# Attention tiles of a mixer layer: one bias-and-minimum pass, one cast and one subtraction per tile over shared PSUM rows, normalising a tile later, some loads in another order

## The chip, the cores and the metric

The kernel runs on one core of one Trainium2 chip. The metric is the device time of one execution in microseconds (us); lower is better. The time before is the median of three runs.

## The reference, cut to what matters

One layer of a hybrid backbone over 2048 latent tokens (a 32 x 64 grid, 1024 channels) and 256 context tokens, in float32. After a norm and modulation, one input projection gives eight column groups. Four of them feed neighbourhood attention with 8 heads of 64 channels: every latent query sees a clamped 8 x 16 window of the grid, with a learned bias, and all context keys, in one softmax:

```python
s_loc = einsum('bhrqd,bhrkd->bhrqk', qr, kg) * scale + bias[None]
s_loc = where(mask, s_loc, -inf)
s_ctx = einsum('bhrqd,bhcd->bhrqc', qr, k_ctx) * scale
p = softmax(concatenate([s_loc, s_ctx], axis=-1), axis=-1)
o = einsum('bhrqk,bhrkd->bhrqd', p_loc, vg) + einsum('bhrqc,bhcd->bhrqd', p_ctx, v_ctx)
y_na = merge(o) * silu(na_g)
```

The other four groups feed a retention path. Both results go through one output projection, a gated residual and a final norm.

## The kernel before, in words

The program has three stages. From 0 to about 562 us it makes the modulation and the projections of keys, values, gates and queries, and stores them in DRAM. From 562 to 1068 us it runs the attention, and fills the gaps of TensorE with projections of the retention path (the "fill": `fill(n)` advances a generator by n steps of three or six matmuls, lines L351 and L362). After that come the retention and the output projection.

The attention has 128 tiles: 8 heads h, 4 row blocks i, 4 column blocks j, tile number t = 16h + 4i + j, and 128 queries in each. A tile has nk = 288, 384 or 512 local keys (12 or 16 grid rows by 24 or 32 grid columns) and 256 context keys. Every float32 operand of a matmul is kept as a high and a low part (`hl`), so each product is made of two or three matmuls. The loop `for t in range(NT + 3)` (L958) writes each engine's order out by hand, as a software pipeline:

- `s_mm(t)`: TensorE makes the scores, local ones in `pl` (two buffers), context ones in `pc`, one PSUM tile of two halves that tiles t and t+1 share.
- a third of the fill, then `s_min(t)`: VectorE copies the context scores to SBUF with their minimum (L752), then adds the bias to the local ones with the minimum of both (L754). Scores carry the opposite sign, so the minimum stands for the softmax's maximum.
- `p_tr(t-2)`: TensorE transposes the probabilities of tile t-2 into `tl` and `tcx` (L773, L776), and ScalarE casts both to the high part in `pt` (L778, L779).
- `s_exp(t)`: ScalarE takes the exponential with its sum (L759).
- `p_lo(t-2)`: VectorE subtracts to get the low part (L786, L787).
- `s_norm(t)`: VectorE takes the reciprocal of the sum (L764), GpSimd multiplies the tile by it (L765).
- a third of the fill, `pv(t-3)`: the products with the values into `po` (L797, L799). On every second tile `combine` adds the four quarters of `po`: ScalarE copies one half (L817), VectorE adds (L818), GpSimd adds twice more (L821), and at the end of a row block of an odd head GpSimd multiplies by the gate (L825).
- the rest of the fill, then, for later tiles, the biases on GpSimd (`bias`, L719 and L722) and the loads.

All loads of this stage are issued by one queue, that of SyncE (SP), in program order: queries (`load_q`, L697), keys (L683), eight groups of value rows per head with six buffers (`load_v`, L705, four transfers a group), gates (`load_gate`, L807), biases (L691), and the fill's own: weights (`st`, L169), rotary tables (L405 and L435) and two reloads of spilled blocks (`hhi`, `hlo`, L673). A load that waits for its buffer holds up all that stand behind it. Stores are issued by ScalarE's queue. The order of the value loads stands in a table:

```python
for g in {(0, 1): (3,), (0, 3): (4,), (1, 1): (5,), (1, 3): (6,), (2, 3): (7,)}.get((i, j), ()):
    load_v(hd, (g,))
```

Group 3 takes the buffer of group 5 of the head before, which that head's last tile reads in its `pv`, three iterations after its scores.

Of the kernel before, what the change touches and what calls it, by code (L numbers as in the profile page):

```python
# [76 lines left out]
def hybrid_kernel(ctx: ExitStack, tc: tile.TileContext, a: dict, out: bass.AP):  # L77
# [526 lines left out]
    psl = pool(pax, "psl", 2, space=PSUM)  # L604
    psc = pool(pax, "psc", 1, space=PSUM)

# [73 lines left out]
    def load_head(h):  # L680
# [6 lines left out]
        return dict(k2=k2, vh=vh, vc=vc, nb={}, vt={}, q={})  # L687
# [25 lines left out]
    def bias(hd, rt, ct):  # L713
# [7 lines left out]
        t = mp.tile([P, kr, cw], F32, name=f"nb{int(rt == 1)}{ct}")  # L721
        nc.gpsimd.tensor_tensor(t, mcol[:, ct, ec:ec + cw].unsqueeze(1).to_broadcast([P, kr, cw]),  # L722
                                hd["ep"][:, :, ec:ec + cw], ALU.subtract)
        hd["nb"][rt, ct] = t
# [7 lines left out]
    def s_mm(t):  # L732
        h, i, j, kr0, kr, kc0, cw = dims(t)
        hd, nk = heads[h], kr * cw
        if t % 2 == 0:
            tl_st["pc"] = psc.tile([P, 2, LC], F32, name="pc")
        pc = tl_st["pc"][:, t % 2, :]
        pl = psl.tile([P, 512], F32, name="pl")
# [5 lines left out]
        sp = ap_.tile([P, 768], F32, name="sp", bufs=3)  # L744
        st = ap_.tile([P, 4], F32, name="stt", bufs=4)
        tl_st[t] = dict(pl=pl, pc=pc, sp=sp, st=st, nk=nk)

    def s_min(t):
        h, i, j = dims(t)[:3]
        T = tl_st[t]  # L750
        sp, st, nk = T["sp"], T["st"], T["nk"]
        nc.vector.tensor_scalar(sp[:, nk:nk + LC], T["pc"], 1.0, None, ALU.mult, ALU.min, accum_out=st[:, 0:1])  # L752
        nb = heads[h]["nb"][RTYPE[i], CTYPE[j]].rearrange("p a b -> p (a b)")
        nc.vector.tensor_tensor_reduce(sp[:, :nk], T["pl"][:, :nk], nb, 1.0, st[:, 0:1], ALU.add, ALU.min, st[:, 1:2])  # L754

    def s_exp(t):
        T = tl_st[t]
        sp, st, n = T["sp"], T["st"], T["nk"] + LC
        nc.scalar.activation(sp[:, :n], sp[:, :n], AF.Exp, bias=st[:, 1:2], scale=-1.0, accum_out=st[:, 2:3])  # L759

    def s_norm(t):
        T = tl_st[t]
        sp, st, n = T["sp"], T["st"], T["nk"] + LC
        nc.vector.reciprocal(st[:, 3:4], st[:, 2:3])  # L764
        nc.gpsimd.tensor_scalar(sp[:, :n], sp[:, :n], st[:, 3:4], 0.0, ALU.mult, ALU.add)  # L765

    def p_tr(t):
# [3 lines left out]
        tl = psl.tile([P, 4, P], F32, name="tl", bufs=1)  # L771
        for g in range(ng_):
            nc.tensor.transpose(tl[:cn, g, :], sp[:, g * cn:(g + 1) * cn], ident)  # L773
        tcx = psc.tile([P, 2, P], F32, name="tcx")
        for g in range(2):
            nc.tensor.transpose(tcx[:, g, :], sp[:, nk + g * P:nk + (g + 1) * P], ident)  # L776
# [3 lines left out]
        T.update(tl=tl, tcx=tcx, pt=pt)  # L780

    def p_lo(t):
        h, i, j, kr0, kr, kc0, cw = dims(t)
        T = tl_st[t]
        pt, ng_, cn = T["pt"], kr // 4, 4 * cw
        nc.vector.tensor_tensor(pt[:cn, :ng_, 1, :], T["tl"][:cn, :ng_, :], f(pt)[:cn, :ng_, 0, :], ALU.subtract)  # L786
        nc.vector.tensor_tensor(pt[:, 4:, 1, :], T["tcx"], f(pt)[:, 4:, 0, :], ALU.subtract)  # L787

    def pv(t):
        h, i, j, kr0, kr, kc0, cw = dims(t)  # L790
        T, hd = tl_st[t], heads[h]
        pt, ng_, cn = T["pt"], kr // 4, 4 * cw
# [557 lines left out]
```

## Time and profile before

| | |
|---|---|
| three runs, median (lowest to highest) | 1419.59 us (1414.53 to 1420.13) |
| profiled execution, first to last instruction | 1413.8 us |
| TensorE busy | 1346.2 us (95%) |
| VectorE, ScalarE, GpSimd busy | 670.2, 553.4, 614.5 us |
| attention stage, 562 to 1068 us: TensorE busy | 473.38 of 506 us |

The profile is of one execution. The page gives its span and no other time of it; the median of the runs lies 5.8 us above the span, for what lies around the first and the last instruction and for the spread between runs. Busy time is that of each engine's instructions; idle time is put down to what ended it.

### The profile page before, as it was taken

How to read it: one execution, taken by the hardware profiler on the slowest of the kernel's cores; microseconds unless marked ns; L12 is line 12 of the kernel's file. 1: busy time of each engine (PE TensorE's matmuls, PEld its weight loads, DVE VectorE, ACT ScalarE, POOL GpSimd, SP SyncE). 2: the span in 40 equal slices, each digit the busy share in tenths (PEclk: the TensorE clock that was granted, in tenths of full speed). 3: DMA queues.
4: the chain of work that ended last, by engine and by line, in shares of the span. 5: the costliest groups of instructions: out<-in, count | busy, mean ns of one | idle time of the engine just before them, and what ended most of it. 6: DMA issues, size and time to landing. Idle time of an engine off the chain costs nothing.

```text
span 1413.8 us, 23044 instructions
## 1 busy us (share of the span) xinstructions
PE 1346.2 (95%) x8380; PEld 1175.6 (83%) x8380; DVE 670.2 (47%) x1563; ACT 553.4 (39%) x1283; POOL 614.5 (43%) x703
## 2 busy tenths in 40 slices
PE   6989999999999999999899988798999999999997
PEld 2467899988887888998799878598999879888886
DVE  5786111100021131677777767577673644344445
ACT  4454212212212221765466544356563234333332
POOL 4452302112201221676777746477673155454342
PEclk9999999999999999999999999999999999999999
DMA  9543666233244577557557585847436997555433
GB/s 310 168 164 133 215 219 231 92 110 104 90 147 159 202 266 218 141 156 196 158 155 174 162 241 167 227 124 191 134 115 203 295 310 258 188 168 174 154 117 127
DMA packets 203634, 253.20 MB, mean 179 GB/s; under 512 B 13057, under 2 KB 151425, under 8 KB 202498
## 3 DMA queue, kind: packets, MB, share of 16 engines
q1 hardware_dynamic: 168098, 186.98, 45.2%
q10 hardware_dynamic: 35424, 64.76, 12.7%
q8 instruction: 66, 1.08, 0.3%
q14 instruction: 46, 0.38, 0.1%
HBM read 168.86 MB, written 82.84 MB: 178 GB/s over the span
## 4 chain that ended last, share of the span: by engine, by line
PE 73%; DMA 10%; DVE 8%; ACT 3%; POOL 2%; issue 2%; SPq 1%; ACTq 0%; DVEq 0%; POOLq 0%
PE mm L351 24%; PE mm L362 19%; PE mm L1193 11%; PE po L797 2%; PE tl L773 2%; PE pl L742 2%; PE mm L916 2%; DMA t<-in_rot_s_dram 2%; DMA q<-qS 2%; PE pc L743 1%; PE po L799 1%; PE tcx L776 1%; PE mm L295 1%; DMA t<-in_rot_k_dram 1%; PE mm L1105 1%
## 5 line engine op out<-in xcount | busy, mean ns | idle before, releaser
L351 PE MATMUL mm<-hhi,whi 128*128 128x512 f32 x640 | 259.6, 406 | 0.0
L351 PE MATMUL mm<-hlo,whi 128*128 128x512 f32 x640 | 253.4, 396 | 5.6 <-DVE hlo L264 2.2
L351 PE MATMUL mm<-hhi,wlo 128*128 128x512 f32 x640 | 253.3, 396 | 0.3 <-DVE wlo L332 0.3
L362 PE MATMUL mm<-whi,hhi 128*128 128x256 f32 x768 | 224.6, 292 | 0.0
L362 PE MATMUL mm<-wlo,hhi 128*128 128x256 f32 x768 | 216.7, 282 | 2.7 <-POOL wlo L332 2.7
L362 PE MATMUL mm<-whi,hlo 128*128 128x256 f32 x768 | 216.1, 281 | 0.0
L332 POOL TENSOR_TENSOR wlo<-st,whi 128x256 fp32r<-128x256 f32 (+1 forms) x97 | 112.4, 1176 | 225.4 <-ACT whi L330 225.2
L765 POOL TENSOR_SCALAR sp<-sp,stt 128x640 f32<-128x640 f32 (+2 forms) x128 | 103.6, 810 | 105.4 <-DVE stt L764 79.6
L362 PEld LDWEIGHTS mm<-wlo,hhi 128*128 128x128 f32 x768 | 145.0, 189 | 3.4 <-POOL wlo L332 3.3
L351 PEld LDWEIGHTS mm<-hlo,whi 128*128 128x128 f32 x640 | 120.8, 189 | 31.3 <-issue 3.3
L362 PEld LDWEIGHTS mm<-whi,hhi 128*128 128x128 f32 x768 | 145.2, 189 | 1.1
L362 PEld LDWEIGHTS mm<-whi,hlo 128*128 128x128 f32 x768 | 145.3, 189 | 0.0
L351 PEld LDWEIGHTS mm<-hhi,whi 128*128 128x128 f32 x640 | 120.9, 189 | 29.1 <-issue 4.6
L351 PEld LDWEIGHTS mm<-hhi,wlo 128*128 128x128 f32 x640 | 120.5, 188 | 29.4 <-DVE wlo L332 0.7
L759 ACT ACTIVATE sp<-sp,stt 128x640 f32<-128x640 f32 (+2 forms) x128 | 107.9, 843 | 51.8 <-DVE stt L754 51.3
L778 ACT CAST pt<-tl 96x384 fp32r<-96x384 f32 (+3 forms) x128 | 67.9, 531 | 150.6 <-PE tl L773 137.2
L786 DVE TENSOR_TENSOR pt<-tl,pt 96x384 fp32r<-96x384 f32 (+3 forms) x128 | 79.4, 620 | 44.5 <-ACT pt L778 43.8
L1193 PE MATMUL mm<-wor,y 128*128 128x512 f32 x384 | 95.6, 398 | 1.5 <-DVE xt L1202 1.1
L742 PE MATMUL pl<-k,q 128*128 128x384 f32 (+2 forms) x256 | 83.3, 346 | 7.1 <-DMA q<-qS 7.1
L1193 PE MATMUL mm<-won,y 128*128 128x512 f32 x336 | 89.9, 406 | 0.0
L743 PE MATMUL pc<-k,q 128*128 128x256 f32 x256 | 72.1, 286 | 16.8 <-DVE sp L752 16.7
L1193 PEld LDWEIGHTS mm<-wor,y 128*128 128x128 f32 x384 | 69.9, 188 | 17.7 <-issue 3.4
(220 smaller groups left out, 2639.1 us busy)
## 6 DMA issues: line engine op xcount, KB each, us to landing
st<-in_w_in_dram SPq DMA_DIRECT2D x48, 512.0 KB
q<-qS SPq DMA_DIRECT2D x64, 256.0 KB
vS<-o ACTq DMA_DIRECT2D x18, 512.0 KB
k<-kS SPq DMA_DIRECT2D x16, 576.0 KB
kS<-o SPq DMA_DIRECT2D x16, 512.0 KB
woS<-g ACTq DMA_DIRECT2D x32, 256.0 KB
qS<-o ACTq DMA_DIRECT2D x16, 512.0 KB
vt<-vS SPq DMA_DIRECT2D x128, 64.0 KB
```

What stands on the lines that cost most here:

```text
L332: eng.tensor_tensor(l, r, f(h), ALU.subtract)
L351: nc.tensor.matmul(pm[:, :n], ww[:, k, cs], h[:, k, :], start=(k == 0 and i == 0), stop=(k == KC - 1 and i == 2))
L362: nc.tensor.matmul(pm[:, t * WG:(t + 1) * WG], h[:, k, o:o + P], ww[:, k, :], start=(k == 0 and i == 0), stop=(k == KC - 1 and i == 2))
L742: nc.tensor.matmul(pl[:, :nk], qa, kg[:, kr0:kr0 + kr, kc0:kc0 + cw], start=(hl == 0), stop=(hl == 1))
L743: nc.tensor.matmul(pc, qa, hd["k2"][:, L:], start=(hl == 0), stop=(hl == 1))
L759: nc.scalar.activation(sp[:, :n], sp[:, :n], AF.Exp, bias=st[:, 1:2], scale=-1.0, accum_out=st[:, 2:3])
L765: nc.gpsimd.tensor_scalar(sp[:, :n], sp[:, :n], st[:, 3:4], 0.0, ALU.mult, ALU.add)
L773: nc.tensor.transpose(tl[:cn, g, :], sp[:, g * cn:(g + 1) * cn], ident)
L778: nc.scalar.copy(pt[:cn, :ng_, 0, :], tl[:cn, :ng_, :])
L786: nc.vector.tensor_tensor(pt[:cn, :ng_, 1, :], T["tl"][:cn, :ng_, :], f(pt)[:cn, :ng_, 0, :], ALU.subtract)
L797: nc.tensor.matmul(po[:, t % 2, :, :], hd["vt"][kr0 // 4 + g][:cn, j, :], pt[:cn, g, :, :], start=(g == 0), stop=False)
L1193: nc.tensor.matmul(pm, yy[:, k, :], ww[:, k, sl], start=(k == 0 and i == 0), stop=(k == 3 and i == 2))
```

## The change

Only the attention stage changes.

- **Scores.** One PSUM tile `sS` of 1536 columns takes the place of `pl` and `pc`. An even tile lies in columns 512-nk to 768, local scores first; an odd tile in 768 to 1024+nk, context first. So each tile's scores are one run of columns, and the context parts of an even and an odd tile share columns 512 to 1024. The four matmuls are the same; the two local ones come first, then the two of the context.
- **Bias and minimum.** The bias tiles of three column types lie in one long tile, with 256 zeros between them, so that one pass adds bias or zero to all columns and takes the minimum.
- **Transposes.** `tr` takes the place of `tl` and `tcx`; one cast and one subtraction cover all groups (rows that no transpose wrote are zeroed once).
- **Normalising.** `s_norm(t-1)` stands right behind `s_mm(t)`, so an iteration later than before.
- **Combine.** ScalarE copies 256 columns in place of 512, VectorE adds twice, with 256 columns each, and GpSimd's two additions go. The product of the two low parts is no longer added. The gate is multiplied in place in `y2`, which is stored.
- **Loads and buffers.** Value group 3 is loaded at tile (0, 3) of a head in place of (0, 1), group 4 at (1, 0), behind the queries, in place of (0, 3); the gate at column block 3 in place of 1. Gate and bias sources (`gt`, `rpbe`) have one buffer each in place of two.

```diff
-    psl = pool(pax, "psl", 2, space=PSUM)
     psc = pool(pax, "psc", 1, space=PSUM)
+    sS = psc.tile([P, 3 * 512], F32, name="sS")
+    tr = psc.tile([P, 6, P], F32, name="tr")
+    nc.vector.memset(tr, 0.0)
+    nbz, nbt = [], {}
+    for big, (edge, full) in enumerate(((288, 384), (384, 512))):
+        z = mp.tile([P, 2 * edge + full + 2 * LC], F32, name=f"nb{big}")
...
-        hd["e"] = kp.tile([P, 16, 32], F32, name="rpbe")
+        hd["e"] = kp.tile([P, 16, 32], F32, name="rpbe", bufs=1)
...
-        for hl in range(2):
-            qa = hd["q"][i][:, hl, j * P:(j + 1) * P]
-            nc.tensor.matmul(pl[:, :nk], qa, kg[:, kr0:kr0 + kr, kc0:kc0 + cw], start=(hl == 0), stop=(hl == 1))
-            nc.tensor.matmul(pc, qa, hd["k2"][:, L:], start=(hl == 0), stop=(hl == 1))
+        for o, k in ((pl, kg[:, kr0:kr0 + kr, kc0:kc0 + cw]), (pc, hd["k2"][:, L:])):
+            for hl in range(2):
+                nc.tensor.matmul(o, hd["q"][i][:, hl, j * P:(j + 1) * P], k, start=(hl == 0), stop=(hl == 1))
...
-        nc.vector.tensor_scalar(sp[:, nk:nk + LC], T["pc"], 1.0, None, ALU.mult, ALU.min, accum_out=st[:, 0:1])
-        nb = heads[h]["nb"][RTYPE[i], CTYPE[j]].rearrange("p a b -> p (a b)")
-        nc.vector.tensor_tensor_reduce(sp[:, :nk], T["pl"][:, :nk], nb, 1.0, st[:, 0:1], ALU.add, ALU.min, st[:, 1:2])
+        n, big = T["nk"] + LC, int(RTYPE[i] == 1)
+        o = nbt[big, CTYPE[j]] - T["lo"]
+        nc.vector.tensor_tensor_reduce(T["sp"][:, :n], T["s"], nbz[big][:, o:o + n], 1.0, 3e38, ALU.add, ALU.min, T["st"][:, 0:1])
...
-        nc.scalar.copy(pt[:cn, :ng_, 0, :], tl[:cn, :ng_, :])
-        nc.scalar.copy(pt[:, 4:, 0, :], tcx)
+        nc.scalar.copy(pt[:, :ng_ + 2, 0, :], tr[:, :ng_ + 2, :])
...
-        nc.vector.tensor_tensor(pt[:cn, :ng_, 1, :], T["tl"][:cn, :ng_, :], f(pt)[:cn, :ng_, 0, :], ALU.subtract)
-        nc.vector.tensor_tensor(pt[:, 4:, 1, :], T["tcx"], f(pt)[:, 4:, 0, :], ALU.subtract)
+        nc.vector.tensor_tensor(pt[:, :n, 1, :], tr[:, :n, :], f(pt)[:, :n, 0, :], ALU.subtract)
...
-        gts[t // 4] = ap_.tile([P, 512], F32, name="gt")
+        gts[t // 4] = ap_.tile([P, 512], F32, name="gt", bufs=1)
...
-        nc.scalar.copy(tmp[fin], po[oth])
-        nc.vector.tensor_tensor(tmp[fin], po[fin], tmp[fin], ALU.add)
-        yv = ys[i][fin].rearrange("p (r w c) -> p r w c", r=8, w=4)
-        for jj in range(2):
-            nc.gpsimd.tensor_tensor(yv[:, :, 2 * jp + jj, :], tmp[fin, jj, 0, :].rearrange("p (r c) -> p r c", r=8),
-                                    tmp[fin, jj, 1, :].rearrange("p (r c) -> p r c", r=8), ALU.add)
+        nc.scalar.copy(tmp[fin], po[oth, :, 0, :])
+        nc.vector.tensor_tensor(tmp[fin], po[fin, :, 0, :], tmp[fin], ALU.add)
+        yv = ys[i][fin].rearrange("p (r w c) -> p w r c", r=8, w=4)[:, 2 * jp:2 * jp + 2]
+        nc.vector.tensor_tensor(yv, po[fin, :, 1, :].rearrange("p j (r c) -> p j r c", r=8),
+                                tmp[fin].rearrange("p j (r c) -> p j r c", r=8), ALU.add)
...
-            nc.gpsimd.tensor_tensor(gt, y2, gt, ALU.mult)
+            nc.gpsimd.tensor_tensor(y2, y2, gt, ALU.mult)
...
             s_mm(t)
+        if 0 <= t - 1 < NT:
+            s_norm(t - 1)
         fill(part[0])
...
-        if t < NT:
-            s_norm(t)
         fill(part[1])
...
-        if h % 2 == 1 and j == 1:
+        if h % 2 == 1 and j == 3:
             load_gate(t)
...
-        for g in {(0, 1): (3,), (0, 3): (4,), (1, 1): (5,), (1, 3): (6,), (2, 3): (7,)}.get((i, j), ()):
+        for g in {(0, 3): (3,), (1, 0): (4,), (1, 1): (5,), (1, 3): (6,), (2, 3): (7,)}.get((i, j), ()):
```

## Rows read from the trace of the kernel before

**Rows 1.** The page: the span, and busy time of each engine.

```profile
span 1413.8 us, 23044 instructions
PE 1346.2 (95%) x8380; PEld 1175.6 (83%) x8380; DVE 670.2 (47%) x1563; ACT 553.4 (39%) x1283; POOL 614.5 (43%) x703
```

**Rows 2.** Windows: stretch, length, busy of PE, PEld, DVE, ACT, POOL, granted clock, DMA.

```profile
562.00:1068.00 506.00, 473.38 (x3537) 446.42 (x3536) 354.32 (x1045) 283.53 (x673) 336.14 (x449) 0.99 0.61 166
655.00:705.00 50.00, 45.29 (x278) 37.90 (x278) 36.97 (x105) 27.82 (x66) 39.59 (x51) 1.00 0.60 170
825.00:862.00 37.00, 26.74 (x164) 23.02 (x163) 19.79 (x58) 13.00 (x29) 14.60 (x22) 0.95 0.73 200
889.00:920.00 31.00, 20.50 (x115) 16.77 (x115) 15.84 (x44) 9.68 (x22) 11.84 (x15) 0.89 0.79 208
```

**Rows 3.** Waits of PE in the attention stage: total us, times, longest us.

```profile
PE pc L743 <- DVE sp L752: 16.7, 6, 8.0
PE pl L742 <- DMA q<-qS: 7.1, 5, 2.7
PE tl L773 <- DVE pt L786: 5.7, 4, 3.8
```

**Rows 4.** Waits of DVE in the attention stage.

```profile
DVE o L412 <- DMA t<-in_rot_s_dram: 13.2, 3, 8.3
DVE o L448 <- DMA t<-in_rot_k_dram: 9.6, 3, 5.3
```

**Rows 5.** Waits of the SP queue in the attention stage.

```profile
SPq L705 <- PE po L799: 84.8, 20, 8.4
```

**Rows 6.** Timeline of the SP queue: start, us, line, transfer, count.

```profile
799.57 1.13 SPq L697 DMA_DIRECT2D q<-qS  x2
808.70 2.46 SPq L705 DMA_DIRECT2D vt<-vS  x4
...
832.64 0.38 SPq L435 DMA_DIRECT2D t<-in_rot_k_dram  x1
```

**Rows 7.** Groups of instructions by line and shape: busy us, mean ns, idle before.

```profile
L752 DVE TENSOR_SCALAR_CACHE_REDUCE sp<-pc 128x256 f32<-128x256 f32 x128 | 53.6, 419 | 23.1 <-PE pc L743 17.2 <-POOL nb L722 2.2 <-POOL sp L765 1.1
...
L787 DVE TENSOR_TENSOR pt<-tcx,pt 128x256 fp32r<-128x256 f32 x128 | 52.7, 412 | 0.0
...
L779 ACT CAST pt<-tcx 128x256 fp32r<-128x256 f32 x128 | 48.0, 375 | 0.0
L818 DVE TENSOR_TENSOR cmb<-po,cmb 64x512 f32<-64x512 f32 x64 | 44.1, 688 | 33.6 <-ACT cmb L817 33.5
...
L754 DVE CUSTOM_DVE_ANT_0 sp<-pl,nb,stt 128x384 f32<-128x384 f32 x64 | 39.6, 618 | 3.2
...
L786 DVE TENSOR_TENSOR pt<-tl,pt 128x512 fp32r<-128x512 f32 x32 | 22.0, 689 | 10.6 <-ACT pt L778 10.6
L764 DVE RECIPROCAL stt<-stt 128x1 f32<-128x1 f32 x128 | 21.0, 164 | 21.0 <-ACT sp L759 16.3
...
L778 ACT CAST pt<-tl 128x512 fp32r<-128x512 f32 x32 | 18.8, 586 | 40.8 <-PE tl L773 39.2 <-PE tcx L776 1.4
```

**Rows 8.** Timeline of PE: an even tile's first matmul, the odd tile's wait.

```profile
853.46 0.37 PE L742 MATMUL pl<-k,q 128*128 128x288 f32 x1 [2.74 <-DMA q<-qS]
...
858.20 0.38 PE L743 MATMUL pc<-k,q 128*128 128x256 f32 x1 [1.07 <-DVE sp L752]
```

**Rows 9.** Timeline of POOL around tile 26 (third row block of an odd head).

```profile
661.05 0.91 POOL L765 TENSOR_SCALAR sp<-sp,stt 128x768 f32<-128x768 f32 x1 [0.54 <-DVE stt L764]
662.28 1.28 POOL L451 TENSOR_TENSOR o<-o 128x512 f32<-128x512 f32 x1 [0.32 <-DVE o L450]
...
664.33 0.88 POOL L821 TENSOR_TENSOR y<-cmb 64x128 f32<-64x128 f32 x2
665.29 1.28 POOL L825 TENSOR_TENSOR gt<-y,gt 128x512 f32<-128x512 f32 x1
666.53 0.81 POOL L722 TENSOR_TENSOR nb<-mcol,ep 128x288 f32<-128x288 f32 x1
```

**Rows 10.** Timeline of PE: the transposes of tile 26.

```profile
664.99 0.60 PE L773 MATMUL tl<-ident,sp 128*128 128x128 f32 x4
```

More of the change, by code (lines that the diff above doesn't have):

```diff
@@ L603, in hybrid_kernel @@
     pax = ExitStack()
-    psl = pool(pax, "psl", 2, space=PSUM)
     psc = pool(pax, "psc", 1, space=PSUM)
+    sS = psc.tile([P, 3 * 512], F32, name="sS")
[4 more added lines that the diff above has]
+        z = mp.tile([P, 2 * edge + full + 2 * LC], F32, name=f"nb{big}")
+        nbz.append(z)
+        at = (0, edge + LC, edge + full + 2 * LC)
+        for o in at[1:]:
+            nc.gpsimd.memset(z[:, o - LC:o], 0.0)
+        for ct, o in enumerate(at):
+            nbt[big, ct] = o
     dmas, chop = [], []
@@ L720, in bias @@
                                     mrow[:, rt, er:er + kr].unsqueeze(2).to_broadcast([P, kr, 32]), ALU.subtract)
-        t = mp.tile([P, kr, cw], F32, name=f"nb{int(rt == 1)}{ct}")
-        nc.gpsimd.tensor_tensor(t, mcol[:, ct, ec:ec + cw].unsqueeze(1).to_broadcast([P, kr, cw]),
+        t, o = nbz[int(rt == 1)], nbt[int(rt == 1), ct]
+        nc.gpsimd.tensor_tensor(t[:, o:o + kr * cw].rearrange("p (a b) -> p a b", b=cw),
+                                mcol[:, ct, ec:ec + cw].unsqueeze(1).to_broadcast([P, kr, cw]),
                                 hd["ep"][:, :, ec:ec + cw], ALU.subtract)
-        hd["nb"][rt, ct] = t
     heads, ys, tl_st = {}, {}, {}
@@ L733, in s_mm @@
         h, i, j, kr0, kr, kc0, cw = dims(t)
[L734 to L738, printed above, removed]
-        kg = hd["k2"][:, :L].rearrange("p (r c) -> p r c", c=GW)
-        for hl in range(2):
-            qa = hd["q"][i][:, hl, j * P:(j + 1) * P]
-            nc.tensor.matmul(pl[:, :nk], qa, kg[:, kr0:kr0 + kr, kc0:kc0 + cw], start=(hl == 0), stop=(hl == 1))
-            nc.tensor.matmul(pc, qa, hd["k2"][:, L:], start=(hl == 0), stop=(hl == 1))
-        sp = ap_.tile([P, 768], F32, name="sp", bufs=3)
-        st = ap_.tile([P, 4], F32, name="stt", bufs=4)
-        tl_st[t] = dict(pl=pl, pc=pc, sp=sp, st=st, nk=nk)
+        hd, nk, odd = heads[h], kr * cw, t % 2
+        pl = sS[:, 1024:1024 + nk] if odd else sS[:, 512 - nk:512]
+        pc = sS[:, 768:1024] if odd else sS[:, 512:768]
+        kg = hd["k2"][:, :L].rearrange("p (r c) -> p r c", c=GW)
+        for o, k in ((pl, kg[:, kr0:kr0 + kr, kc0:kc0 + cw]), (pc, hd["k2"][:, L:])):
+            for hl in range(2):
+                nc.tensor.matmul(o, hd["q"][i][:, hl, j * P:(j + 1) * P], k, start=(hl == 0), stop=(hl == 1))
+        tl_st[t] = dict(s=sS[:, 768:1024 + nk] if odd else sS[:, 512 - nk:768], nk=nk, lo=LC * odd, co=nk * (1 - odd),
+                        sp=ap_.tile([P, 768], F32, name="sp", bufs=3), st=ap_.tile([P, 4], F32, name="stt", bufs=4))
     def s_min(t):
@@ L758, in s_exp @@
         sp, st, n = T["sp"], T["st"], T["nk"] + LC
-        nc.scalar.activation(sp[:, :n], sp[:, :n], AF.Exp, bias=st[:, 1:2], scale=-1.0, accum_out=st[:, 2:3])
+        nc.scalar.activation(sp[:, :n], sp[:, :n], AF.Exp, bias=st[:, 0:1], scale=-1.0, accum_out=st[:, 1:2])
     def s_norm(t):
@@ L798, in pv @@
         for g in range(2):
-            nc.tensor.matmul(po[:, t % 2, :, :], hd["vc"][:, g, :], pt[:, 4 + g, :, :], start=False, stop=(g == 1))
+            nc.tensor.matmul(po[:, t % 2, :, :], hd["vc"][:, g, :], pt[:, ng_ + g, :, :], start=False, stop=(g == 1))
         del tl_st[t]
@@ L815, in combine @@
             ys[i] = ap_.tile([P, 512], F32, name="y2", bufs=4)
-        tmp = ap_.tile([P, 2, 2, P], F32, name="cmb", bufs=1)
-        nc.scalar.copy(tmp[fin], po[oth])
-        nc.vector.tensor_tensor(tmp[fin], po[fin], tmp[fin], ALU.add)
-        yv = ys[i][fin].rearrange("p (r w c) -> p r w c", r=8, w=4)
-        for jj in range(2):
-            nc.gpsimd.tensor_tensor(yv[:, :, 2 * jp + jj, :], tmp[fin, jj, 0, :].rearrange("p (r c) -> p r c", r=8),
-                                    tmp[fin, jj, 1, :].rearrange("p (r c) -> p r c", r=8), ALU.add)
+        tmp = ap_.tile([P, 2, P], F32, name="cmb", bufs=1)
+        nc.scalar.copy(tmp[fin], po[oth, :, 0, :])
[3 more added lines that the diff above has]
+                                tmp[fin].rearrange("p j (r c) -> p j r c", r=8), ALU.add)
         if h % 2 == 1 and jp == 1:
             gt, y2 = gts.pop(t // 4), ys[i]
-            nc.gpsimd.tensor_tensor(gt, y2, gt, ALU.mult)
-            y_put(h // 2, i // 2, (i % 2) * 512, gt, 2)
+            nc.gpsimd.tensor_tensor(y2, y2, gt, ALU.mult)
+            y_put(h // 2, i // 2, (i % 2) * 512, y2, 2)
     def run(n):
```

20 lines of the change are left out of this document (8 added, 12 removed).

## The prediction

> **What bounds the kernel now.** I read the page's engine shares first: TensorE is busy 1346.2 of 1413.8 us, 95%, and no other engine reaches half [rows 1]. The change leaves every matmul in place, so it can only win what TensorE loses in the attention stage. I therefore cut that stage out in windows. Of its 506 us TensorE is busy 473.4, so 32.6 us are idle [rows 2]: that is the purse. VectorE with 354, GpSimd with 336 and ScalarE with 284 us are far from full.
>
> The idle time is not spread evenly. 37.0 - 26.7 = 10.3 us lie in 825 to 862, 31.0 - 20.5 = 10.5 us in 889 to 920, 50.0 - 45.3 = 4.7 us in 655 to 705; a single wait of 3.8 us is the longest behind the low-part subtraction [rows 2, 3]. In the first two stretches the granted clock is 0.95 and 0.89 of the full 2.4 GHz, 1.0 or 0.99 elsewhere [rows 2]: behind a long gap TensorE runs for a while at the low level. That is up to 37 x 0.05 + 31 x 0.11 = 5.3 us more, of which part falls on idle time.
>
> TensorE's waits name VectorE's pass over the context scores (16.7 us, the longest 8.0), then late queries (7.1) [rows 3]. But VectorE is not slow there. Its own waits show it standing before rotary tables of the fill, 13.2 and 9.6 us, the longest 8.3 [rows 4]; the pass that TensorE waits for is queued behind them. So the root is lateness of transfers. The queue that issues them, SP, itself waits 84.8 us for buffers of the value loads [rows 5]. One such wait is plain in its timeline: queries go out at 799.57, are issued by 800.70, and the next value load only at 808.70, 8.0 us later [rows 6].
>
> **The change part by part.** *VectorE, ScalarE, GpSimd.* From 256 to 512 columns the subtraction grows from 412 to 689 ns, 1.08 ns a column, and the cast from 375 to 586, 0.82 ns [rows 7]. A tile of 640 columns has 384 + 256.
> - Bias and minimum: before 419 + 618 = 1037 ns; the merged pass, by the subtraction's slope since no row shows it at that width, 618 + 256 x 1.08 = 895. Saves 0.14 us, 18 us over 128 tiles.
> - Subtraction: the second one's start-up goes, 412 - 256 x 1.08 = 136 ns: 17 us.
> - Cast: 375 - 256 x 0.82 = 165 ns: 21 us of ScalarE.
> - Combine: one addition of 688 ns becomes two of 256 columns, about 2 x 412: 0.14 us more, 64 times, 9 us of VectorE. GpSimd loses two additions, 0.88 us [rows 9], 64 times, 56 us; ScalarE's copy shrinks likewise.
> - Reciprocal: the same instruction, but an iteration later its sum is ready, so its 21.0 us of idle time [rows 7] mostly go.
>
> Net VectorE does 26 us less of 354, GpSimd 56 of 336, ScalarE over 21. By itself this is worth nothing, as all of it runs beside TensorE's matmuls. It counts where these engines are late: in 655 to 705, where VectorE is busy 37 of 50 us and TensorE idles 4.7. I take 3 us there (bounds 0 and 4.7). The memsets at the start run on engines that have little to do and precede the first transposes by two iterations: nothing, at worst their own microsecond or two.
>
> *The loads.* Value group 3 now stands behind the point at which its buffer comes free. Its wait, 8.0 us in the example, held up what stood behind, in part loads that were due then; those are issued earlier by at least its own issue time of 2.5 us and at most 8.0 + 2.5 = 10.5 [rows 6]. Group 4 now stands behind the queries it preceded, and gates behind tables they preceded. Against this, the gate and bias buffers are halved, so SP also waits for GpSimd to have read them; by the program's order both have been read about an iteration before, so I cost this at nothing, and at a delay of the next loads by a GpSimd backlog of an instruction or two if not. In the two gaps around 840 and 910 and in the 3.8 us wait, 24.6 us are idle. Transfers there are not only issued late: DMA is busy 0.73 and 0.79 of the time [rows 2], so an earlier issue is partly an earlier place in a full queue. The rotary table of rows 6 went out at 832.64; 8.3 us of waiting at most [rows 4] against a shift of 2.5 to 10.5. I take 4 us in the first gap, 5 in the second and 2 in the third, 11 of 24.6 (bounds 0 and 24.6), and 2 of the 5.3 us of clock.
>
> *The shared score tile.* The context matmul of an odd tile already waits for the pass over the even tile's half, though it writes other columns: the even tile starts at 853.46, and the odd one's `pc` waits 1.07 us for L752 [rows 8]. The new row shares its middle in the same way, and now the wait is for the whole merged pass, 895 in place of 419 ns, so 0.48 us longer, while the second local matmul comes ahead of it and hides a part. Six such waits are shown [rows 3]: 6 x 0.48 = 2.9 us. I take 1.5 (bounds 0 and 2.9 plus as much for tiles that now just make it).
> The Trainium skill, "PSUM — Partial Sum Buffer", section "PSUM bank collisions raise a hardware error", has the rule behind this: engines have to be kept apart by bank and quadrant, not by address. The trace agrees with rows 8. Without the rule the context matmul would wait only for tile t-2, and the 16.7 us of rows 3 would move to the next wait, the transposes'; with it the sum has the 1.5 us of loss.
>
> *Normalising a tile later.* This adds a wait. In GpSimd's queue the multiplication now stands behind everything of the iteration before: fill, gate, bias. Tile 26 shows the price. Before, it is normalised at 661.05, and its transposes start at 664.99 [rows 9, 10]. Now it follows the bias that ends at 666.53 + 0.81 = 667.34, less 0.96 for the additions that go (664.33 to 665.29), since the instruction at 662.28 waited for VectorE and moves little: 666.38, plus 0.91, is 667.29. The transposes are 2.3 us late, and TensorE with them. Gates occur on 16 tiles: bounds 0 and 16 x 2.3 = 37 us. This stretch is crowded, GpSimd works without a pause from 662.28 on; over the stage it is busy 66% and will be 55%. So I price the 16 nearer the lower end, a third of a microsecond each: 5 us.
>
> **The sum.** 3 + 11 + 2 - 1.5 - 5 = 9.5 us less: span 1413.8 to 1404.3. The median lies 5.8 us above the span, so I forecast 1410 us.
>
> **Rivals.**
> - *The loads were the whole trouble.* Transfers arrive in time, TensorE's gaps close, and GpSimd, 56 us lighter, is never late. For it: rows 4 and 5. Against it: DMA at 0.73 to 0.79. Three quarters of 32.6 + 5.3 us: 28 less, 1391.5.
> - *The transfers are as late as before.* The reloads of spilled blocks fill the queue whatever the order, and 3 us from lighter engines pay for the new waits: 1419, no change. For it: the DMA share in the gaps; against it: the 8.0 us in which SP issues nothing.
> - *Slower: GpSimd becomes the last wait.* Norm behind gate and bias delays the transposes. My gains are 16 us; at 1 us for each of the 16 gate tiles they are used up, from there on it decides. At the 2.3 us of tile 26 on all: 37 + 1.5 - 16, 22 slower, 1442; at 1.5 us 1429. Against it: before, TensorE's list has no such wait of weight, and 56 us go.
>
> **How the numbers follow.** Forecast, 3 to 17 us less: 0.50. First rival 0.15, second 0.21, third 0.14. The runs lie 5.6 us apart and half a percent is 7.1 us, about what can be told from no change: faster means under 1412.5, slower over 1426.7. Of the forecast's 0.50 some 0.36 lie under 1412.5, with the first rival 0.51; the second and the rest, with the mild end of the third, make 0.36 the same; 0.13 slower. The range leaves out the best third of the first rival's spread and most of the third: 1395 to 1425. The forecast's own range is 1402 to 1417.
>
> **What would show it.** Right: the idle time in the stage falls from 32.6 to about 20 to 25 us; SP's wait for `po` shrinks; waits for rotary tables fall to half; `pc` waits for the merged pass a half microsecond longer each, at both parities; the merged pass takes about 895 ns at 640 columns; small waits of the transposes for GpSimd's multiplication appear on odd heads. Wrong: transposes waiting for it by over 16 us in all; rotary tables as late as before with the DMA share up; or a gate load that comes late and stops GpSimd's queue, and with it the next tile's normalising.

## The result, and the profile after

The changed kernel takes 1422.77 us in the median of 20 runs (1417.69 to 1431.88), the kernel before, beside it on the same chip, 1416.74 (1412.88 to 1423.43): ratio 1.0045, interval 1.0031 to 1.0060. It is some 6 us slower, where I forecast 9.5 us less. The profiled execution has a span of 1419.1 us and a time of its own of 1420.85, so what lies around the span is 1.8 us; most of the 5.8 us that I added to the span was spread between runs.

The page, span and busy time of each engine, and windows of the stage and of my crowded stretch (columns as in [rows 2]):

```profile
span 1419.1 us, 22560 instructions
PE 1351.0 (95%) x8380; PEld 1181.2 (83%) x8380; DVE 641.2 (45%) x1244; ACT 530.7 (37%) x1155; POOL 560.1 (39%) x579
```

```profile
562.00:1069.00 507.00, 476.57 (x3535) 450.78 (x3534) 324.33 (x724) 260.78 (x545) 281.53 (x323) 0.97 0.61 166
655.00:705.00 50.00, 46.28 (x301) 40.38 (x300) 33.73 (x75) 25.39 (x52) 35.64 (x40) 1.00 0.63 176
```

The three side engines got lighter as worked out: VectorE 670.2 to 641.2, GpSimd 614.5 to 560.1, ScalarE 553.4 to 530.7 [rows 1]. TensorE's idle time in the stage fell by 2 us (507.0 - 476.6 = 30.4), but its granted clock fell from 0.99 to 0.97 [rows 2]. (A difference of a few us between two profiles is one between two single executions; what a part costs is told below by many runs of each kernel.)

An average over the stage hides what happened. Cut at the same tiles (the passes of tiles 0, 32, 64, 96 and 127), before and after, by two heads a window:

```profile
564.00:681.00 117.00, 113.60 (x879) 108.00 (x879) 83.15 (x257) 74.06 (x184) 83.59 (x113) 1.00 0.63 166
681.00:801.00 120.00, 115.92 (x861) 108.56 (x860) 89.25 (x261) 70.29 (x165) 86.93 (x116) 1.00 0.63 167
801.00:942.00 141.00, 119.64 (x835) 109.52 (x834) 94.26 (x273) 63.00 (x144) 78.28 (x103) 0.96 0.66 187
942.00:1058.00 116.00, 112.22 (x868) 108.44 (x868) 82.36 (x244) 71.44 (x170) 83.56 (x115) 0.99 0.55 148
```

```profile
563.00:687.00 124.00, 116.00 (x878) 110.58 (x876) 75.50 (x176) 69.32 (x154) 72.20 (x85) 0.97 0.59 158
687.00:806.00 119.00, 115.82 (x860) 108.72 (x859) 81.86 (x181) 63.95 (x132) 72.35 (x84) 1.00 0.62 167
806.00:941.00 135.00, 120.71 (x843) 111.42 (x841) 87.57 (x196) 57.30 (x112) 64.39 (x71) 0.95 0.69 196
941.00:1059.00 118.00, 113.04 (x868) 109.06 (x867) 74.79 (x165) 65.86 (x139) 69.80 (x83) 0.97 0.54 146
```

Heads 4 and 5, where the load order was to help, take 141 - 135 = 6 us less. Heads 0 and 1 take 7 us more: 8.0 us idle in place of 3.4, at a clock of 0.97 in place of 1.00. Two more us come in the last two heads, and from the last pass to the end of the program it is 359.9 us after, 355.3 before.

TensorE's waits in the stage (total, times, longest), and the load queue's, answer to [rows 3] and [rows 5]:

```profile
PE sS L751 <- DVE stt L760: 13.0, 7, 6.6
PE tr L778 <- POOL sp L771: 10.3, 7, 4.5
PE sS L751 <- DMA q<-qS: 3.6, 1, 3.6
```

```profile
SPq L808 <- POOL y L825: 76.5, 11, 10.3
SPq L716 <- PE po L800: 55.9, 13, 7.5
```

Two rows are new. The transposes wait 10.3 us for GpSimd's multiplication (L771), 0.2 us before. The largest of these seven waits, 4.5 us, is an old one under another name: it is the 3.8 us wait of [rows 3]. Before and after, ScalarE stands at a cast of a weight for the fill until its transfer is in, and TensorE waits for what that holds up (before, then after):

```profile
982.79 0.71 ACT L330 CAST whi<-st 128x256 fp32r<-128x256 f32 x2 [6.94 <-DMA st<-in_w_in_dram]
984.85 0.85 PE L773 MATMUL tl<-ident,sp 128*128 128x128 f32 x4 [3.76 <-DVE pt L786]
```

```profile
982.05 0.40 ACT L330 CAST whi<-st 128x256 fp32r<-128x256 f32 x1 [6.56 <-DMA st<-in_w_in_dram]
985.15 1.11 PE L778 MATMUL tr<-ident,sp 128*128 128x128 f32 x4 [4.54 <-POOL sp L771]
```

So some 6 of the 10.3 us are new. Second, the queue's wait for the values' buffers shrank from 84.8 to 55.9 us, but a gate load (L808) now waits 76.5 us until GpSimd has read the one gate buffer (L825). GpSimd's timeline shows the first kind of wait at the tile from which I took my price, tile 26; TensorE's row follows:

```profile
668.89 1.30 POOL L825 TENSOR_TENSOR y<-y,gt 128x512 f32<-128x512 f32 x1
670.15 0.79 POOL L733 TENSOR_TENSOR nb<-mcol,ep 128x288 f32<-128x288 f32 x1
670.92 0.91 POOL L771 TENSOR_SCALAR sp<-sp,stt 128x768 f32<-128x768 f32 x1
```

```profile
671.88 0.66 PE L778 MATMUL tr<-ident,sp 128*128 128x128 f32 x4 [1.49 <-POOL sp L771]
```

Gate, bias, then the multiplication, and TensorE idle for 1.49 us: the order worked out from [rows 9], at a price of 1.5 in place of 2.3.

### The profile page after: what moved, and what is told of

It is laid out like the page before. It is cut to its first block, busy times and chain, and to the rows that moved or that the text cites. A ratio compares the mean times of both kernels' runs of the same rounds, so it can differ in the third digit from the quotient of the medians.

```text
span 1419.1 us, 22560 instructions
## 1 busy us (share of the span) xinstructions
PE 1351.0 (95%) x8380; PEld 1181.2 (83%) x8380; DVE 641.2 (45%) x1244; ACT 530.7 (37%) x1155; POOL 560.1 (39%) x579
## 4 chain that ended last, share of the span: by engine, by line
PE 73%; DMA 9%; DVE 6%; issue 3%; POOL 3%; ACT 2%; SPq 2%; DVEq 0%; POOLq 0%; ACTq 0%
PE mm L351 25%; PE mm L362 18%; PE mm L1192 11%; PE sS L751 3%; PE tr L778 2%; PE po L798 2%; PE mm L915 2%; DMA k<-kS 2%; PE tr L780 1%; DMA q<-qS 1%; PE po L800 1%; PE mm L295 1%; PE mm L1104 1%; PE mm L1103 1%; PE mm L1102 1%
## 5 line engine op out<-in xcount | busy, mean ns | idle before, releaser
L782 ACT CAST pt<-tr 128x640 fp32r<-128x640 f32 (+1 forms) x128 | 95.6, 747 | 205.4 <-PE tr L780 193.0
L788 DVE TENSOR_TENSOR pt<-tr,pt 128x640 fp32r<-128x640 f32 (+1 forms) x128 | 113.9, 890 | 102.8 <-ACT pt L782 102.1
L771 POOL TENSOR_SCALAR sp<-sp,stt 128x640 f32<-128x640 f32 (+2 forms) x128 | 103.4, 809 | 100.7 <-DVE stt L770 79.8
L760 DVE CUSTOM_DVE_ANT_0 sp<-sS,nb 128x640 f32<-128x640 f32 (+2 forms) x128 | 105.5, 825 | 26.4 <-PE sS L751 20.3
L751 PE MATMUL sS<-k,q 128*128 128x256 f32 (+3 forms) x512 | 100.6, 319 | 16.9 <-DVE stt L760 13.0
L751 PEld LDWEIGHTS sS<-k,q 128*128 128x128 f32 x512 | 84.5, 191 | 24.4 <-DVE stt L760 15.9
```

What stands on the lines that cost most here:

```text
L751: nc.tensor.matmul(o, hd["q"][i][:, hl, j * P:(j + 1) * P], k, start=(hl == 0), stop=(hl == 1))
L760: nc.vector.tensor_tensor_reduce(T["sp"][:, :n], T["s"], nbz[big][:, o:o + n], 1.0, 3e38, ALU.add, ALU.min, T["st"][:, 0:1])
L771: nc.gpsimd.tensor_scalar(sp[:, :n], sp[:, :n], st[:, 2:3], 0.0, ALU.mult, ALU.add)
L782: nc.scalar.copy(pt[:, :ng_ + 2, 0, :], tr[:, :ng_ + 2, :])
L788: nc.vector.tensor_tensor(pt[:, :n, 1, :], tr[:, :n, :], f(pt)[:, :n, 0, :], ALU.subtract)
```

## The experiments

All were timed in five rounds beside the kernel before, whose median lay between 1417.9 and 1421.4 us. Each ratio has an interval of 0.002 to 0.003 to each side (normalising late in the kernel before has 0.0035), so a difference between two of them is known to about 0.003, or 4 us.

| kernel | ratio | interval |
|---|---|---|
| change, normalising back in its old place | 0.9981 | 0.9962, 1.0001 |
| change, second bias of head 0 set earlier | 1.0004 | 0.9984, 1.0025 |
| before + normalising late | 1.0124 | 1.0089, 1.0159 |
| before + load order | 0.9954 | 0.9933, 0.9974 |
| ... + one gate and one bias source buffer | 1.0083 | 1.0057, 1.0109 |
| before + load order + combine | 0.9933 | 0.9908, 0.9959 |
| ... + joint transposes' tile | 0.9934 | 0.9912, 0.9957 |
| ... + shared score row | 0.9954 | 0.9932, 0.9975 |
| ... + one bias source buffer | 0.9931 | 0.9900, 0.9963 |
| ... + one gate buffer, product in place | 0.9952 | 0.9932, 0.9971 |
| ... + normalising late | 0.9974 | 0.9955, 0.9993 |
| ... + one bias source, seven value buffers | 0.9931 | 0.9909, 0.9953 |
| change, normalising back, bias earlier | 0.9981 | 0.9963, 0.9999 |
| change, normalising back, pass split in two | 0.9995 | 0.9978, 1.0013 |
| change, two gate buffers | 1.0015 | 0.9993, 1.0037 |
| change, two gate buffers, normalising back | 0.9982 | 0.9962, 1.0003 |
| change, its control with one gate buffer | 0.9993 | 0.9973, 1.0014 |
| change, normalising back, gate on ScalarE's queue | 1.0046 | 1.0024, 1.0068 |

**Two parts alone: the load order, and normalising late.** First undone in the changed kernel, then each alone in the kernel before.

```diff
# normalising back in its old place
             s_mm(t)
-        if 0 <= t - 1 < NT:
-            s_norm(t - 1)
...
             p_lo(t - 2)
+        if t < NT:
+            s_norm(t)
```

> The changed kernel with the normalising back in its old place, in the tile's own iteration behind the low-part subtraction; all else as changed. Theory A (normalising a tile later is what costs: 10.3 us of transposes waiting for GpSimd, and the slow clock behind the gaps): 6 to 10 us less than the changed kernel, so 0 to 4 us under the kernel before, the waits of the transposes for GpSimd gone and the clock drop at 570 us gone. Rival B (the merged pass, which holds the shared score row longer, costs): within 3 us of the changed kernel, with TensorE's waits for the pass still near 13 us. Rival C (the gate's single buffer holds up the SP queue): within 3 us of the changed kernel.

> The kernel before with one edit: normalising a tile later. Theory A: 5 to 10 us slower than before, with new waits of the transposes for GpSimd of 10 us or more (GpSimd has 56 us more to do here than in the changed kernel) and more low clock. Rivals B and C: within 3 us of before.

> The kernel before with one edit: the new order of value and gate loads, gates still in two buffers. If the order is what closes gaps around 840 and 910 us: 3 to 8 us less than before and waits for rotary tables down by half. If the transfers come as late as before whatever the order: within 2 us of before.

The load order gains 0.46%, 6.5 us, and normalising late costs 1.24% in the kernel before, where the transposes wait for GpSimd 27 times, and the difference of 0.64% in the changed one. So both parts count, and neither is all: with normalising back the changed kernel stands at 0.998, not at the load order's 0.995. Two things were not as expected. With the load order alone VectorE's waits for rotary tables did not fall by half, but from 22.8 [rows 4] to 17.4 us:

```profile
DVE o L412 <- DMA t<-in_rot_s_dram: 12.4, 2, 7.4
DVE o L448 <- DMA t<-in_rot_k_dram: 5.0, 2, 3.7
```

And in the profile with normalising back the transposes no longer wait for GpSimd, but TensorE waits 23.7 us for the merged pass in place of 13.0, and from the first to the last pass it takes 494.1 us in place of 495.9. So the gain of 0.64% stands in the medians; these two executions show little of it.

**The start of the stage.** In the changed kernel's first microseconds the first tile's multiplication stands behind the bias in GpSimd's queue; TensorE idles 1.5 us up to 567.9 and 1.4 us up to 570.8, and its granted clock falls to 0.66 over the next ten microseconds. The second of the two waits:

```profile
570.79 0.88 PE L778 MATMUL tr<-ident,sp 128*96 128x128 f32 x3 [1.35 <-POOL sp L771]
```

I set head 0's second bias earlier, in the loop ahead of the attention.

```diff
+        if n == 1:
+            for ct in range(3):
+                bias(heads[0], 1, ct)
...
-        if i == 0 and j < 3:
+        if h > 0 and i == 0 and j < 3:
             bias(hd, 1, j)
```

> The changed kernel with the second set of biases of head 0 made before the loop, so that GpSimd's queue is empty when the first tiles are normalised; all else as changed. Theory A: the 1.35 us wait of the first transposes goes, with it the clock drop after 570 us (0.66 in that stretch): 3 to 5 us less than the changed kernel. Rival (the drop at the start comes from the 1.5 us wait for the merged pass alone): clock still low there, under 2 us less.

> The changed kernel with normalising back in its old place and the second bias of the first head set before the loop. If the clock's fall at the start of the stage (567 to 580 us) costs time of its own, and the bias removes it as it did with normalising late (1.0004 against 1.0045), this gives 0.994 to 0.996. If that fall costs nothing that shows in the total, it stays at 0.998, as with normalising back alone.

The window of 570 to 580 us, of the changed kernel and then of that with the bias earlier:

```profile
570.00:580.00 10.00, 9.21 (x55) 9.19 (x56) 3.16 (x7) 4.33 (x10) 9.38 (x13) 0.66 0.19 56
```

```profile
570.00:580.00 10.00, 10.00 (x86) 10.00 (x85) 5.17 (x12) 7.34 (x18) 6.94 (x10) 1.00 0.36 99
```

In this stretch TensorE is busy without a gap at the full clock (its one wait just ahead of it, 2.2 us for the merged pass, ends at 569.7); head 0, from its first pass to that of head 1, takes 57.0 us in place of 60.7 (56.4 before), and the ratio falls by 0.41%. With normalising back the same edit gains nothing. So a part of the price of normalising late arises in this one place. How much is not settled: head 0 says 3.7 us by these two profiles, but 1.6 us by the changed kernel against itself with normalising back (60.7 and 59.1).

**The buffers that were halved.** The 4 x 256 zeros in the bias tiles take 4 kB of a partition, as much as the two buffers that went.

```diff
# load order, and then:
-        hd["e"] = kp.tile([P, 16, 32], F32, name="rpbe")
+        hd["e"] = kp.tile([P, 16, 32], F32, name="rpbe", bufs=1)
...
-        gts[t // 4] = ap_.tile([P, 512], F32, name="gt")
+        gts[t // 4] = ap_.tile([P, 512], F32, name="gt", bufs=1)
```

> The kernel before with the new load order, and with one gate buffer and one bias source buffer in place of two. The load order alone gave 0.9954. Theory 'the single buffers hold up the load queue': the gate load waits some 70 us in all for GpSimd's multiplication, rotary tables come late again, and the ratio goes back to 0.998 to 1.000. Rival 'single buffers cost nothing, as forecast': 0.995 to 0.996, and TensorE's list in the stage is that of the load order alone.

In the kernel before, one gate buffer with one bias source buffer takes away the load order's gain and 12 us more. There the product is stored from the gate's own tile, so the next gate load waits for the store as well (SyncE's queue in the stage):

```profile
SPq L807 <- DMA yS<-gt: 107.0, 12, 11.3
```

Head 1 takes 69.2 us there, 58.8 with the load order alone. The changed kernel multiplies in the output tile, so this is an upper end. I then gave the changed kernel two gate buffers; the room came from the combine, which adds in the output tile without its temporary, and a control has that alone.

```diff
-        gts[t // 4] = ap_.tile([P, 512], F32, name="gt", bufs=1)
+        gts[t // 4] = ap_.tile([P, 512], F32, name="gt")
...
-        tmp = ap_.tile([P, 2, P], F32, name="cmb", bufs=1)
-        nc.scalar.copy(tmp[fin], po[oth, :, 0, :])
-        nc.vector.tensor_tensor(tmp[fin], po[fin, :, 0, :], tmp[fin], ALU.add)
...
+        po4 = po.rearrange("p j u (r c) -> p j u r c", r=8)
+        nc.scalar.copy(yv, po4[oth, :, 0])
+        nc.vector.tensor_tensor(yv, po4[fin, :, 0], yv, ALU.add)
...
```

> The changed kernel with two gate buffers again; the room comes from the combine, which adds in place in the output tile, without its temporary. Theory 'the single gate buffer ties the load queue to the multiplication and takes back what the load order won': the queue's 76.5 us of waiting for the multiplication go, and the ratio falls from 1.0045 by about 0.006 to 0.998 or 0.999. Rival 'the queue would only wait elsewhere, for the values' buffers': the wait moves to the value loads (over 75 us there) and the ratio stays at 1.003 to 1.005.

> Two gate buffers and normalising back in its old place. If the two losses add up, 0.998 less 0.006: 0.991 to 0.993. If the gate's buffer is no loss once normalising is back, 0.997 to 0.999.

> The control of the run with two gate buffers: the combine without its temporary, and normalising in its old place, but one gate buffer. Every theory so far expects what normalising back alone gave, 0.997 to 0.999; a value outside that would mean that the combine in place has a price or a gain of its own.

> Normalising in its old place, one gate buffer, and the gate's load issued by ScalarE's queue, at the same place of the program. If the loss is that a waiting gate load holds up the other loads in SyncE's queue, not that the gate comes late, this wins it back with one buffer: 0.991 to 0.993. If the gate coming late, or room for transfers, is what costs, 0.997 to 0.999; if ScalarE, standing before the gate load, is itself late, its exponentials come late and it is 1.000 or more.

```diff
-        nc.sync.dma_start(gts[t // 4], gS[h // 2][:, i * 512:(i + 1) * 512])
+        nc.scalar.dma_start(gts[t // 4], gS[h // 2][:, i * 512:(i + 1) * 512])
```

Two buffers give 0.30% (1.0045 to 1.0015) and, with normalising back, 0.11% (0.9993 to 0.9982): half or less of what I expected; the second is what I had named for 'no loss once normalising is back'. Moving the load to ScalarE's queue made it worse, 1.0046 against 0.9981. There SyncE's queue no longer stands at the gate, but it stands 78.0 us at the values' buffers, in place of 48.4. Head 1 takes 60.9 us in place of 63.8, so there the queue is freed; but head 3 takes 63.6 in place of 58.0. There ScalarE's cast of a weight for the fill waits 6.25 us for a transfer, up to 778.74, and TensorE 3.90 us, up to 780.98, for what that holds up. That the freed queue put other loads ahead of the weights is likely, and was not tried by itself.

**One part at a time.** Load order and combine alone give 0.9933, the best so far; to that I added the other parts singly. The edits are the lines of the change, part by part; the combine is the changed one, in which the product of the two low parts is not added.

> The kernel before with the new load order and the new combine (ScalarE copies 256 columns, VectorE adds twice, GpSimd not at all; the product of the two low parts is left out as in the changed kernel). Theory 'lighter GpSimd is worth nothing while it is not waited for': 0.995 to 0.996, as with the load order alone, or 1 to 2 us worse for VectorE's added 9 us. Rival 'GpSimd's backlog delays transposes and gates': 0.992 to 0.993.

> The kernel before with load order and new combine (0.9933), and of the rest only the joint transposes' tile with one cast and one subtraction. Theory 'it only saves VectorE and ScalarE time beside TensorE': 0.992 to 0.994. Rival 'the first transpose now waits for the whole subtraction, and the values' products for the whole cast': TensorE's waits at the transposes and at the values' products grow by 3 us or more, 0.996 or more.

> Load order and new combine (0.9933), and of the rest only the shared score row and its order of matmuls, both local ones ahead of the context ones, read by two passes as before. Theory 'the row is what the rest costs': a second score tile can be begun no earlier, TensorE's waits for the passes grow from 13.8 us to over 18, 0.996 to 0.998. Rival 'the row costs nothing by itself': 0.992 to 0.994.

> Load order and new combine (0.9933), with one buffer for the source of the biases in place of two. SyncE's queue then waits for GpSimd's last use in the head before, 5 us in the changed kernel. Theory 'the two single buffers cost by holding the queue, and this one little': 0.993 to 0.995. If this is the dear one, 0.998 or more.

> Load order and new combine (0.9933), with one gate buffer, and the gate multiplied in place in the output tile, as the changed kernel has it (with the product stored from the gate's own tile a single buffer gave 1.0083, with the bias source's buffer halved too). Theory 'the single gate buffer holds the load queue for some 75 us and loses part of what the load order won': 0.997 to 0.999. Rival 'held up for the multiplication alone it costs nothing, only the wait for the store did': 0.992 to 0.995.

```diff
# the row alone, over two passes
-        pc = tl_st["pc"][:, t % 2, :]
-        pl = psl.tile([P, 512], F32, name="pl")
+        pl = sS[:, 1024:1024 + nk] if odd else sS[:, 512 - nk:512]
+        pc = sS[:, 768:1024] if odd else sS[:, 512:768]
...
# the gate's buffer alone
-        gts[t // 4] = ap_.tile([P, 512], F32, name="gt")
+        gts[t // 4] = ap_.tile([P, 512], F32, name="gt", bufs=1)
...
-            nc.gpsimd.tensor_tensor(gt, y2, gt, ALU.mult)
+            nc.gpsimd.tensor_tensor(y2, y2, gt, ALU.mult)
```

The joint transposes' tile (one cast, one subtraction) and the single bias source buffer change nothing. The combine's 0.9933 lies at the edge of what I expected if GpSimd's backlog delayed others. The shared row and the single gate buffer cost 0.2% each, which by itself is no more than the uncertainty, and for the gate it is nearer the rival's range (0.992 to 0.995) than mine; but both have a mark in the trace. For the gate it is head 1, the first with gates. SyncE's queue, with one gate buffer and then with two:

```profile
656.16 0.58 SPq L691 DMA_DIRECT2D rpbe<-in_rpb_e_dram  x1
665.20 0.34 SPq L807 DMA_DIRECT2D gt<-gS  x1
...
669.12 0.36 SPq L405 DMA_DIRECT2D t<-in_rot_s_dram  x1
```

```profile
655.32 0.59 SPq L691 DMA_DIRECT2D rpbe<-in_rpb_e_dram  x1
656.13 0.34 SPq L807 DMA_DIRECT2D gt<-gS  x1
...
662.55 0.42 SPq L405 DMA_DIRECT2D t<-in_rot_s_dram  x1
```

The gate goes out 9 us later and the rotary table behind it 6.6 us later. With one buffer, VectorE then stands 4.40 us for that table, and TensorE 3.18 us for VectorE (of VectorE's timeline one row, of TensorE's the other):

```profile
675.89 0.69 DVE L412 TENSOR_TENSOR o<-mm,t 64x512 f32<-64x512 f32 x1 [4.40 <-DMA t<-in_rot_s_dram]
```

```profile
678.39 0.39 PE L743 MATMUL pc<-k,q 128*128 128x256 f32 x1 [3.18 <-DVE sp L752]
```

With normalising in its old place, head 1 takes 57.9 to 60.1 us in the eight profiles with two gate buffers and both loads in SyncE's queue (the kernel before included), and 62.3 to 64.5 us in the five with one buffer whose product is stored from the output tile. So there the delay is plain, some 4 us; later heads return it (in the pair of these rows 486.8 against 486.2 us from the first to the last pass). And it does not add to the price of normalising late, which falls on the same head: with load order and combine head 1 takes 58.4 us, with normalising late added 62.0, with one gate buffer added 62.7, and in the changed kernel, which has both, 62.9, or 61.9 with two gate buffers.

For the row the mark is the place of the wait. TensorE's longest stall, with load order and combine, which has the two score tiles, and with the row alone added to them:

```profile
907.74 0.58 PE L743 MATMUL pc<-k,q 128*128 128x256 f32 x1 [8.76 <-DVE sp L752]
```

```profile
910.78 1.65 PE L742 MATMUL sS<-k,q 128*128 128x512 f32 x4 [8.12 <-DVE stt L753]
```

In the first one local matmul has been made, and the first context one (`pc`, 256 columns) waits. In the second all four of the tile wait, though the local ones write columns that no pass reads at that time. So no local matmul is done ahead of the stall any more. The stall itself has not grown (8.1 us against 8.8). TensorE's waits for the passes grow from 13.8 to 19.1 us, as expected if the row costs, but its other waits fall, and all its waits in the stage are 25.4 and 26.9 us.

The pass was also split again in the changed kernel, over the same row:

```diff
...
-        nc.vector.tensor_tensor_reduce(T["sp"][:, :n], T["s"], nbz[big][:, o:o + n], 1.0, 3e38, ALU.add, ALU.min, T["st"][:, 0:1])
+        nc.vector.tensor_scalar(T["sp"][:, co:co + LC], T["s"][:, co:co + LC], 1.0, None, ALU.mult, ALU.min, accum_out=st[:, 3:4])
+        nc.vector.tensor_tensor_reduce(T["sp"][:, lo:lo + nk], T["s"][:, lo:lo + nk], nbz[big][:, o:o + nk], 1.0, st[:, 3:4], ALU.add, ALU.min, st[:, 0:1])
```

> The changed kernel with normalising back in its old place, and the merged pass split again into two (context first, then local with the bias) over the same shared row. Theory 'the merged pass holds the shared row and the exponential longer when VectorE is late': TensorE's waits for it shrink from 23.7 us to under 18 and the ratio falls to 0.996 or less. Rival 'the merged pass only saves VectorE time': waits as before or longer, VectorE some 18 us busier, 0.998 to 1.000.

It brought nothing (0.9995 against 0.9981; the waits for the pass 23.8 us, as before), so no cost of its length is seen.

**GpSimd's queue, and a seventh value buffer** (`bufs=7` for `vt`, one for `rpbe`).

> The kernel before with load order and new combine (0.9933), and normalising a tile later. In the kernel before, with GpSimd's 56 us of additions, normalising late cost 1.2%; in the changed kernel, without them, 0.6%. Theory 'the price is GpSimd's queue ahead of the multiplication, and the additions were part of that queue': 0.999 to 1.001, with TensorE's waits for the multiplication near 10 us. Rival 'the price does not depend on what else GpSimd does': 1.005 to 1.006, with waits of 20 us or more.

> Load order, new combine and one bias source buffer (0.9931), and the 2 kB that this frees used for a seventh buffer of the value groups. If SyncE's wait for the values' buffers (71.7 us) is what still makes queries and rotary tables late, that wait falls under 50 us and the ratio to 0.989 to 0.991. If the transfers themselves are now the limit, 0.992 to 0.994.

Normalising late costs 0.41% on top of load order and combine, a third of the 1.24% in the kernel before and less than either range that I had named; TensorE's waits for it, without and with GpSimd's 56 us of additions, are:

```profile
PE tl L773 <- POOL sp L765: 24.5, 27, 2.9
```

```profile
PE tl L773 <- POOL sp L765: 13.9, 8, 5.0
```

(The first row is the kernel before with normalising late, the second load order, combine and normalising late. In the second row 5.0 of the 13.9 us are again the wait behind the weight, up to 982.89.) So the price depends on what else stands in GpSimd's queue, as I had it. The seventh value buffer took the queue's wait for values from 71.7 to 11.2 us and gained nothing, as I had named it for transfers that are themselves the limit: TensorE still waits 6.4 us for VectorE at 907.24, and VectorE 15.3 us for rotary tables. A long wait of the load queue is not by itself the lateness that counts.

## Why the prediction was wrong

- **VectorE, ScalarE, GpSimd lighter: 3 us.** Not refuted. The sizes were within a tenth (merged pass at 640 columns 817 ns, forecast 895; additions 422, forecast 412). The combine gives 0.21%, 3 us, on the load order, with an uncertainty as large; the joint cast and subtraction give nothing, as work beside TensorE should.
- **Load order: 11 us and 2 of clock.** This step failed by its size. The place was right, but it gives 6.5 us alone, half of 13, and 6 us in heads 4 and 5 of the changed kernel. TensorE's single waits in the first gap add up to 10.2 us before, 6.0 with the load order alone and 6.4 in the changed kernel, where I had 4 less; in the second to 10.2, 7.1 and 6.6, where I had 5 less; the third, behind the weight, is 3.8, 3.0 and 4.5, where I had 2 less. The clock did not recover: over these two heads it is 0.96 before, 0.94 with the load order alone and 0.95 in the changed kernel. The step had it that loads issued earlier arrive earlier for those who wait. VectorE's waits for rotary tables (22.8 us before, 17.4 with the load order alone) fell in the changed kernel to 9.9 us, or 15.2 with one at the same line, in the first gap, whose end the profile does not name:

```profile
DVE o L412 <- DMA t<-in_rot_s_dram: 7.0, 2, 5.9
DVE o L412 <- issue: 5.3, 1, 5.3
...
DVE o L448 <- DMA t<-in_rot_k_dram: 2.9, 1, 2.9
```

In the second gap the sine table shows why the order won so little. Its issue and VectorE's use of it, before and with the load order alone:

```profile
904.05 0.33 SPq L405 DMA_DIRECT2D t<-in_rot_s_dram  x1
914.11 0.69 DVE L412 TENSOR_TENSOR o<-mm,t 64x512 f32<-64x512 f32 x1 [8.34 <-DMA t<-in_rot_s_dram]
```

```profile
897.59 0.43 SPq L405 DMA_DIRECT2D t<-in_rot_s_dram  x1
906.56 0.69 DVE L412 TENSOR_TENSOR o<-mm,t 64x512 f32<-64x512 f32 x1 [7.37 <-DMA t<-in_rot_s_dram]
```

It goes out 1.7 us before VectorE comes to it, and with the new order 1.6 us; from its issue to its use it takes 10.1 and 9.0 us. So for VectorE, which waits, it went out no sooner than before, and the whole of the wait lies between its issue and its arrival.

- **Gate and bias buffers: nothing.** This step failed for the gate. I reasoned that its reader is an iteration behind "by the program's order"; but the load queue runs ahead of the engines, and a load that waits for its buffer takes that lead from all that stand behind it: 76.5 us of waits in the queue, and 4 us in head 1 with normalising in its old place. In the whole it costs 0.30, 0.11 and 0.19% in the three pairs, in the mean 0.20%, 2.8 us, each pair within its own uncertainty. The bias source costs nothing.
- **Shared score tile: 1.5 us.** Measured 0.21%, 3 us, with an uncertainty as large; my bounds were 0 to 5.8. I had the local matmuls go ahead of the wait and hide a part; the wait stands ahead of them. I had cited the Trainium skill, "PSUM — Partial Sum Buffer", section "PSUM bank collisions raise a hardware error", on keeping engines apart by bank. By the 512 float32 columns that the page gives a bank, the local matmuls write another bank than the pass before reads, so the rule does not ask for this wait; the trace has it. What sets it, no run here tells.
- **Normalising a tile later: 5 us.** Right in size. Four pairs with the light combine give 0.64, 0.23, 0.33 and 0.41%, in the mean 0.40%, 5.7 us. The place was half right: in the changed kernel tile 26 (1.5 us) as worked out, but as much at the starts of head 0 (1.4 us, with the clock behind it) and head 1 (1.8 us, up to 633.65), which have no gate but a bias ahead of the multiplication. So the third rival, GpSimd as the last wait, holds in kind; its 5.7 us are a third of the 16 at which I had it decide, and it came out slower because the gains were smaller than I had them.

The sum by measured terms: -3 (combine) - 6.5 (loads) + 3 (row) + 2.8 (gate) + 5.7 (late) = +2 us, against +6 measured. My -9.5 is missed chiefly by the load order's size (6.5 us with its clock) and by the gate's buffer (2.8). The last 4 us are not placed: the merged pass with its zeros was never run without the row, and five differences of this uncertainty don't add up closer. In the two profiles they lie behind the attention: from the first to the last pass the changed kernel takes 1.8 us more, behind the last pass 4.6 more. There TensorE waits 6.0 us for `vw` of ScalarE (1.2 before), but it waits 5.2 with two gate buffers and normalising back, where this end takes 356.9 us, so that alone does not explain it. In the seven profiles with one gate buffer in SyncE's queue and the product in the output tile this end takes 357.9 to 361.6 us, in nine of the eleven with two it takes 353.6 to 357.4 (in the others 359.7 and 363.0). That hints at the gate's buffer; no run tested it.

The best kernels here are the one before with load order and combine (0.9933, 1409.13 us), and the same with one bias source and seven value buffers (0.9931, 1406.84 us).

## What to carry to other kernels

Before halving a buffer, look at who issues its load: in a queue that issues in order, one load that waits for its reader takes away the lead of every load behind it, and the loss shows at other tiles (here a rotary table 6.6 us later, though little of that stayed in the total). When a load is moved forward, compare its issue with the moment at which its reader comes to it: here the sine table of the second gap went out as late for VectorE as before. When a step is moved behind others in an engine's queue, price it where that queue is full, the start of a stage included, and not by the engine's busy share. Bundles of small changes should be run part by part: here two parts gave 0.7% and the rest took it back, and half a percent more.

## What the runs showed that I had not expected

A stall of 1.5 us and another of 1.4 within 3 us, at the start of the stage, cost more than their length: the granted clock was 0.66 of full speed from 570 to 580 us, where the two levels are 1.2 and 2.4 GHz, and head 0 took 3.7 us less once the second stall was gone. The stalls' length alone did not decide it. At the same place one stall of 2.2 us left the clock of that stretch at 1.00 (bias earlier), and so did stalls of 0.8 and 2.0 us within 4 us (normalising late in the kernel before); but with one of 1.8 us it was 0.96 (normalising back) and 0.87 (normalising back, bias earlier).

One product stored from the tile into which the next load goes made a single buffer dear: 107.0 us of waits in the load queue and 1.3% of the time (together with one bias source buffer, which by itself cost nothing), against 69.5 us and 0.2% where the product lies elsewhere.
